# Sums over the partitions in a hybrid residual block: LayerNorm's mean and variance and the first FFN norm's sum by two float32r matmuls instead of one f32 matmul

## The chip, the cores and the metric

The kernel runs on one core of one Trainium2 chip. The metric is device time in microseconds, the median of several runs. The profile names the engines PE (matmul), PEld (weight load, of the same engine), DVE (VectorE), ACT (ScalarE), POOL (GpSimd) and SP (SyncE, which issues DMAs).

## What is computed

One trunk layer on x (1024 positions, 1024 channels), f32 in and out:

```python
h = rms_norm(x, norm_mix_g) * (1.0 + sc1) + sh1
b_s, c_s, v_s, v_c, gl_c, gate_br = split(h @ w_in)
y_a = (b_s * causal_dwconv(c_s * v_s, conv_short_w)) @ w_short_out
u = causal_dwconv(v_c * sigmoid(gl_c), conv_conf_w) + conv_conf_b
y_b = silu(layer_norm(u, conf_ln_g, conf_ln_b)) @ w_conf_out
g_a, g_b = split(sigmoid(gate_br))
x = x + g1 * ((g_a * y_a + g_b * y_b) @ w_o)
h2 = rms_norm(x, norm_ffn_g) * (1.0 + sc2) + sh2
a, bgate = split(h2 @ w_ffn_in)
x = x + g2 * ((silu(a) * bgate) @ w_ffn_out)
return rms_norm(x, final_norm_g)
```

The shifts, scales and gates (sh1, sc1, g1, sh2, sc2, g2) come from a product of silu(c) with w_ada. The change concerns three places where a sum over the channels is needed: the mean and the variance in `layer_norm`, and the sum of squares in the RMSNorm ahead of the FFN.

## The kernel before, in words

Everything is held transposed: channels lie on the 128 partitions (8 blocks of 128, KC = 8), positions on the free axis, in two halves of 512 (H). A product therefore has weights of 128x128 as the stationary side and tiles of 128x512 as the moving side.

Products run in float32r, in three parts. Each operand is split into a high part (a cast on ACT) and a low part (a subtraction on DVE, of some weights on POOL): `split_w` (L220 to L231; casts at L226, subtractions at L227) for weights, `t_split` (L419) and `q_split` (L839; casts L848, subtractions L850) for tiles. `mm3` (L372) then adds high by high (L380), high weight by low tile (L381) and low weight by high tile (L383). Most products save one in eight by a Strassen-like scheme of seven products in the order of PRODUCTS ("1265734"); some operands of these are sums of weight blocks, made at L304. One product of such a set on PE is 24 matmuls.

The stages in order, with where they lie in the trace: the combined input projection, with the causal convolution of width 31 on DVE beside it; from 565 us the fourteen products of `w_short` (`ya_order`, L1045), with LayerNorm on DVE and ACT beside them; the product with `w_conf` (tile `yb`, from 645 us); the product with `w_o` (tile `mix`, from 732 us), whose second half of positions runs beside the first half's FFN norm; the FFN; the last norm.

A sum over channels has two steps: the 8 channel blocks are added up elementwise, and the 128 partitions of the result are then summed by one matmul with a 128x128 tile `ones` as the stationary side, which leaves the sum on every partition of a PSUM tile. Before the change all these sums take the f32 tile as it is, in an f32 matmul. The ones at issue:

- `ln_mean` (L930), behind the first product of `ya_order`, for both halves: `tot[h]`, which POOL adds up at L923, is summed at L934 into a PSUM tile `mu`, and ACT scales it into SBUF at L936. `ln_square` (L941) then subtracts the mean (L945), squares on ACT (L947) and adds up on DVE (L951), for one channel block behind each product.
- `ln_rstd` (L953), behind the eleventh product: `sqs[h]` is summed at L957 into a PSUM tile `var`, for both halves, and the reciprocal root follows (L431 on ACT, L436 to L438 on DVE). `act_b` (L977) uses it, for the operands `zs` of the next product.
- `norm_2_first` (L1119), behind the first `mix` block of the second half: `norm_start` (L536) sums `sums[0]` at L540. `sums[0]` has been added up at L1102 from the squares of L1096.

Tiles come from pools. `mu` and `var` lie in a pool of two PSUM tiles ("ps2"), which the copies `y` (L1025) of the second product of `ya_order` also use. The pool "gs" holds six f32 tiles of 128x512 in SBUF: gates on their way (`ga`, `gb`), squares, reciprocal roots, the tiles `xr` of `mix`, and from L834 on four q tiles (`q01`) that stay until they have been split as q7. A tile that is asked for when all buffers are taken waits for one to come free.

The order of the instructions on each engine is set ahead of the run by a planner: it follows the order of the code, but where an instruction isn't ready by the planner's own model of times, it lets a later one of the same engine past. `tc.issue_after(ins)` pins an instruction behind another one on the same engine. On the chip each engine then goes through its list in order, with semaphores between the engines.

`fill` (L179) is a tile that nothing reads, of FILL f32 columns; it takes up room between the constants and the other pools.

Of the kernel before, what the change touches and what calls it, by code (L numbers as in the profile page):

```python
# [36 lines left out]
F32R = mybir.dt.float32r  # L37
AF = mybir.ActivationFunctionType
ALU = mybir.AluOpType

P = 128
D = 1024
T = 1024
H = 512
# [76 lines left out]
PIECES = [(0, 512), (512, 256), (768, 256)]  # L121


FILL = 248


@with_exitstack
def block_kernel(ctx: ExitStack, tc: tile.TileContext, x0, xT, c, vecs, ada, w_first, w_plain, w_duals,
                 w_short, w_conf, w_o, w_fi, w_fo, w_last, outT):
    nc = tc.nc  # L130

    def pool(name, bufs, **kw):
        return ctx.enter_context(tc.tile_pool(name=name, bufs=bufs, **kw))
# [10 lines left out]
    cp = pool("const", 1)  # L144
# [8 lines left out]
    gsp = pool("gs", 6)  # L153
# [4 lines left out]
    def ps_tile(name):  # L158
        return psp.tile([P, H], F32, tag="ps", name=name)

    def ps2_tile(name):
        return ps2p.tile([P, H], F32, tag="ps2", name=name)

    def hl_tile(name, dt=F32R):
        return tp.tile([P, H], dt, tag="t", name=name)
# [7 lines left out]
    def f32(t):  # L173
        return t.bitcast(F32)
# [3 lines left out]

    nc.gpsimd.memset(fill.tile([P, FILL], F32, name="fill"), 0.0)  # L179

# [2 lines left out]
    cs = cp.tile([P, D], F32, name="cs")  # L183
    ones = cp.tile([P, P], F32, name="ones")
    nc.vector.memset(ones, 1.0)
    eps1 = cp.tile([P, 1], F32, name="eps1")
    nc.vector.memset(eps1, EPS)
    eps2 = cp.tile([P, 1], F32, name="eps2")
# [227 lines left out]
    def t_pair(name):  # L416
        return hl_tile(name + "h"), hl_tile(name + "l")
# [9 lines left out]
    def rstd_start(ss, eps, name, n=H, tile_of=g_tile):  # L427

        r, t = tile_of(name + "r")[:, :n], tile_of(name + "t")[:, :n]
        ss = ss[:, :n]  # L430
        act = nc.scalar.activation(r, ss, AF.Abs_reciprocal_sqrt, bias=eps)  # L431
        return ss, eps, r, t, act.ins

    def rstd_end(ss, eps, r, t, exp):

        nc.vector.scalar_tensor_tensor(out=t, in0=r, scalar=-0.5, in1=r, op0=ALU.mult, op1=ALU.mult)  # L436
        nc.vector.scalar_tensor_tensor(out=t, in0=ss, scalar=eps, in1=t, op0=ALU.add, op1=ALU.mult)
        rstd_end.ins = nc.vector.scalar_tensor_tensor(out=r, in0=t, scalar=1.5, in1=r, op0=ALU.add, op1=ALU.mult).ins  # L438
        return r
# [81 lines left out]
    def squares_x(src, acc=None, clock=(), tile_of=g_tile):  # L521

        for i, t in enumerate(src):
            sq = tile_of("sq")
            act = nc.scalar.activation(sq, t, AF.Square, scale=1.0 / 32.0)
            if acc is None:
                acc = sq
            else:
                add = nc.vector.tensor_tensor(acc, acc, sq, ALU.add)
                if i in clock:  # L530
                    keep_clock(keep_clock.ins, 1, sq)
                    keep_clock(keep_clock.ins, 1, wide=True)
        squares_x.ins = act.ins, add.ins
        return acc

    def norm_start(acc, name, n=H, tile_of=g_tile, ss_tile=ps_tile):  # L536
        ss = ss_tile("ss")
        acc = acc if isinstance(acc, list) else [acc]
        for t in acc:
            norm_start.ins = nc.tensor.matmul(ss[:, :n], ones, t, start=t is acc[0], stop=t is acc[-1]).ins  # L540
        return rstd_start(ss, eps1, name, n, tile_of)
# [20 lines left out]
    def gate(b, j, h, ps):  # L562
        sig = g_tile("sig")
        nc.scalar.activation(sig, ps, AF.Sigmoid)
        nc.scalar.dma_start(gate_dram[b, j][:, halves[h]], sig)

    def keep_clock(ins, n, src=None, wide=False):

        t = ps2_tile("clock")
        lhs, src = (ones_r[:, :P], ones_r) if wide else (ones, ones if src is None else src[:, :P])  # L570
        for _ in range(n):
            with tc.issue_after(ins) if ins else ExitStack():
                ins = nc.tensor.matmul(t[:, : src.shape[-1]], lhs, src, start=True, stop=True).ins
        keep_clock.ins = ins
# [15 lines left out]
    ones_r = s_tile("ones_r", F32R)  # L590
    nc.vector.memset(f32(ones_r), 1.0)
    keep_clock(None, CLOCK[0], wide=True)
    for s, row in zip(halves, c_rows):
        silu = nc.scalar.activation(row[:1], crow[:, s], AF.Silu)
# [331 lines left out]
    tot = [hl_tile(f"tot{h}", dt=F32) for h in range(2)]  # L926
# [3 lines left out]
    def ln_mean():  # L930
        mu = []
        for h in range(2):
            mps = ps2_tile("mu")
            nc.tensor.matmul(mps, ones, tot[h], start=True, stop=True)  # L934
            mu.append(hl_tile(f"mu{h}", dt=F32))
            nc.scalar.activation(mu[h], mps, AF.Copy, scale=1.0 / D)  # L936
        return mu

    sqs = [None, None]
# [13 lines left out]
    def ln_rstd(sqs):  # L953
        rs = []
        for h in range(2):
            var = ps2_tile("var")
            nc.tensor.matmul(var, ones, sqs[h], start=True, stop=True)  # L957
            rs.append(rstd_start(var, eps2, f"rl{h}"))
        return [rstd_end(*r) for r in rs]

# [84 lines left out]
    for i, (d, m) in enumerate(ya_order):  # L1045
        product(ya_banks[d], m, tq[m], ya_evacs[d], onto="2")
        if q_steps:
            q_steps.pop(0)()
        if i == 0:
            mu = ln_mean()  # L1050
        elif i <= KC:
            ln_square(i - 1)
        elif i == KC + 2:
            rl = ln_rstd(sqs)
            act_b(0, 0)
# [9 lines left out]
    for h in range(2):  # L1065
# [3 lines left out]
        gs = []  # L1069
# [34 lines left out]
    def h2_of(k, h, r2, hi_lo=None):  # L1104

        t = x1[k][:, halves[h]]
        nc.vector.scalar_tensor_tensor(out=t, in0=t, scalar=aff2[:, k : k + 1], in1=r2, op0=ALU.mult, op1=ALU.mult)
        if hi_lo:
            hi, lo = hi_lo
            nc.scalar.activation(hi, t, AF.Identity, bias=modc(24 + k))  # L1110
            nc.vector.scalar_tensor_tensor(
                out=lo, in0=t, scalar=modc(24 + k), in1=f32(hi), op0=ALU.add, op1=ALU.subtract
            )
        nc.scalar.activation(t, t, AF.Identity, bias=modc(24 + k))
        return t
# [2 lines left out]
    ts = {m: [None] * (KC // 2) for m in PRODUCTS}  # L1118
    def norm_2_first():  # L1119

        r2 = rstd_end(*norm_start(sums[0], "r2"))
        for k in range(KC):
            ts["12"[k // KH]][k % KH] = hl = t_pair(f"h2{k}")
            h2_of(k, 0, r2, hl)
# [34 lines left out]
    sums = {}  # L1159
    for h in range(2):  # L1160
        for i in range(KC):
            mix(i, h)
            if h == 0:
                load_b(32 + i)
            if (h, i) == (0, KC - 1):
                modulation_of(*loaded.pop())
            if h == 1 and i == 0:
                for k in range(KC):
                    affine(aff2, k, 32, vec, V_GFFN)
                norm_2_first()  # L1170
            if h == 1 and i in S2_AT:
                next(in_units[1]["begin"])
# [121 lines left out]
    ss = ps_tile("ss")  # L1294
    r2 = None
# [6 lines left out]
    r2 = rstd_end(*r2)  # L1302
# [49 lines left out]
    n = 2 * GROUP * P  # L1352
# [98 lines left out]
    for i in range(len(PIECES)):  # L1451
        acc, sqs = sqs[0] if i else None, []
# [84 lines left out]
```

## Time and profile before

| what | value |
|---|---|
| median of 3 runs | 1471.18 us (1470.85 to 1472.19) |
| span of the profiled execution | 1469.8 us; its time outside the profile isn't listed |
| granted PE clock, mean | 0.998 |
| f32 sums of the mean, L934 | 4 records, 571.0 to 572.3 us |
| f32 sums of the variance, L957 | 4 records, 627.3 to 628.8 us |
| f32 sum of the first FFN norm, L540 `ss<-xr` | 2 records, at 781.6 us |

Times within the trace are microseconds from the start of the span. Of an f32 matmul the trace shows two records, each with its own weight load. Records of PE overlap: a matmul is still draining when the next one begins, so what one costs is read from the distance between starts and not from its busy time. A number in brackets behind a row is the engine's idle time ahead of it, and what ended it.

### The profile page before, as it was taken

Reading aid. Unit: us, or ns where it says so; the run is one execution under the profiler, and the core shown is the slowest. Engines: PE = TensorE matmul, PEld = TensorE weight load, DVE = VectorE, ACT = ScalarE, POOL = GpSimd, SP = SyncE. Lnnn points to the kernel's source line nnn. Section 1 sums busy time; section 2 is a strip of 40 time slices with the busy share of each in tenths; the row PEclk is TensorE's granted clock in tenths of the full one; section 3 lists DMA queues with packets and bytes.
Section 4 is the critical chain, followed back from the end, with each engine's and each line's share of the span. In section 5 each row is a group of like instructions: output and inputs, shape, how many; then the busy total and the mean of one; then the engine's idle time right before and its main releaser. Section 6 shows DMA issues by size and latency. Waiting matters only on the chain.

```text
span 1469.8 us, 17768 instructions
## 1 busy us (share of the span) xinstructions
PE 1459.0 (99%) x6447; PEld 1197.9 (81%) x6447; DVE 1178.7 (80%) x1625; ACT 615.0 (42%) x896; POOL 515.7 (35%) x464
## 2 busy tenths in 40 slices
PE   9999999999999999999999999999999999999997
PEld 5888888888888888888888888888888888888887
DVE  8999888887998969999688798777777765676755
ACT  5753433333433346455235474444444443222325
POOL 0046677767777771111022002101111115435005
PEclk9999999999999999999999999999999999999999
DMA  9412213222222258376596336654555449999403
GB/s 373 165 59 72 101 58 129 72 86 101 101 67 78 93 205 303 115 239 215 194 315 221 106 106 233 221 170 163 168 185 173 158 154 373 341 287 280 139 15 115
DMA packets 83913, 247.97 MB, mean 169 GB/s; under 512 B 9665, under 2 KB 11713, under 8 KB 83826
## 3 DMA queue, kind: packets, MB, share of 16 engines
q1 hardware_dynamic: 43072, 138.63, 28.3%
q0 software_dynamic: 37008, 95.63, 19.8%
q10 hardware_dynamic: 3746, 12.59, 2.3%
q8 instruction: 50, 0.82, 0.2%
q14 instruction: 37, 0.30, 0.1%
HBM read 184.41 MB, written 62.39 MB: 168 GB/s over the span
## 4 chain that ended last, share of the span: by engine, by line
PE 97%; DVE 1%; POOL 0%; issue 0%; ACT 0%; POOLq 0%; DVEq 0%
PE bank L383 12%; PE bank L380 12%; PE bank L381 12%; PE x L381 8%; PE x L383 8%; PE x L380 7%; PE z L380 4%; PE z L383 4%; PE z L381 4%; PE y L381 3%; PE y L380 3%; PE y L383 3%; PE mix L383 2%; PE mix L380 2%; PE yb L383 2%; PE yb L380 2%
## 5 line engine op out<-in xcount | busy, mean ns | idle before, releaser
L226 ACT CAST wh<-raw 128x1024 fp32r<-128x1024 f32 (+2 forms) x253 | 255.2, 1010 | 454.9 <-PE bank L381 129.9
L227 POOL TENSOR_TENSOR wl<-raw,wh 128x1024 fp32r<-128x1024 f32 x84 | 204.8, 2446 | 82.1 <-ACT wh L226 82.1
L227 DVE TENSOR_TENSOR wl<-raw,wh 128x1024 fp32r<-128x1024 f32 (+2 forms) x169 | 193.6, 1146 | 37.4 <-ACT wh L226 36.1
L902 DVE SCALAR_TENSOR_TENSOR c<-diff,vec,c 128x512 f32<-128x512 f32 x232 | 171.0, 752 | 4.4
L1250 POOL DMA_DIRECT2D hid<-stage x71 | 37.9, 534 | 345.4 <-DVE stage L421 341.1
L380 PE MATMUL bank<-th,wh 128*128 128x512 f32 x288 | 112.0, 389 | 0.0
L381 PE MATMUL bank<-tl,wh 128*128 128x512 f32 x288 | 112.0, 389 | 0.0
L383 PE MATMUL bank<-th,wl 128*128 128x512 f32 x288 | 112.0, 389 | 0.0
L902 DVE SCALAR_TENSOR_TENSOR c<-u,wsum,c 128x512 f32<-128x512 f32 x112 | 84.3, 753 | 2.6
L420 ACT CAST stage<-g 128x512 fp32r<-128x512 f32 x62 | 38.4, 622 | 84.0 <-DVE g L1239 41.9
L246 POOL TENSOR_TENSOR raw<-raw 128x1024 f32<-128x1024 f32 x12 | 29.2, 2433 | 125.1 <-DVE wl L227 87.7
L421 DVE TENSOR_TENSOR stage<-g,stage 128x512 fp32r<-128x512 f32 x62 | 42.4, 689 | 26.9 <-ACT stage L420 26.8
L381 PEld LDWEIGHTS bank<-tl,wh 128*128 128x128 f32 x288 | 54.1, 188 | 11.3
L383 PEld LDWEIGHTS bank<-th,wl 128*128 128x128 f32 x288 | 54.1, 188 | 11.2
L380 PEld LDWEIGHTS bank<-th,wh 128*128 128x128 f32 x288 | 54.1, 188 | 11.2
L1276 POOL DMA_DIRECT2D th<-hid x71 | 38.1, 537 | 52.8 <-PE x L383 29.3
L380 PE MATMUL x<-th,wh 128*128 128x512 f32 x144 | 56.1, 390 | 0.1
L383 PE MATMUL x<-th,wl 128*128 128x512 f32 x144 | 56.0, 389 | 0.0
L381 PE MATMUL x<-tl,wh 128*128 128x512 f32 x144 | 56.0, 389 | 0.0
L246 DVE TENSOR_TENSOR raw<-raw 128x1024 f32<-128x1024 f32 (+1 forms) x17 | 19.2, 1129 | 42.2 <-DMA raw<-in_w_fi 31.6
L380 PE MATMUL yb<-zsh,wh 128*128 128x512 f32 x128 | 49.8, 389 | 0.0
L381 PE MATMUL yb<-zsl,wh 128*128 128x512 f32 x128 | 49.8, 389 | 0.0
(811 smaller groups left out, 4243.9 us busy)
## 6 DMA issues: line engine op xcount, KB each, us to landing
hid<-stage POOLq DMA_DIRECT2D x71, 512.0 KB, 4.6
raw<-in_w_fi SPq DMA_DIRECT2D x54, 512.0 KB, 4.4
raw<-in_w_duals SPq DMA_DIRECT2D x48, 512.0 KB, 3.5
th<-hid POOLq DMA_DIRECT2D x71, 256.0 KB, 5.7
tl<-hid POOLq DMA_DIRECT2D x71, 256.0 KB, 5.7
ada<-in_ada SPq DMA_DIRECT2D x24, 512.0 KB, 5.5
raw<-in_ada SPq DMA_DIRECT2D x24, 512.0 KB, 4.5
raw<-in_w_fo SPq DMA_DIRECT2D x24, 384.0 KB, 5.8
```

The lines of the kernel that those rows point to most:

```text
L226: hi = nc.scalar.copy(wh, raw)
L227: lo = lo_engine.tensor_tensor(wl, raw, f32(wh), ALU.subtract)
L246: eng.tensor_tensor(a["s1"], a["21"], a["22"], ALU.add)
L380: nc.tensor.matmul(ps, wh, xh, start=first, stop=False, skip_group_check=again)
L381: nc.tensor.matmul(ps, wh, xl, start=False, stop=False, skip_group_check=again)
L383: mm3.ins = nc.tensor.matmul(ps, wl, xh, start=False, stop=last, skip_group_check=again).ins
L420: t_split.act = nc.scalar.copy(hi, src).ins
L421: t_split.ins = nc.vector.tensor_tensor(lo, src, f32(hi), ALU.subtract).ins
L902: tap.ins = nc.vector.scalar_tensor_tensor(out=out, in0=src[:, s : s + H], scalar=wt, in1=acc, op0=ALU.mult, op1=ALU.add).ins
L1250: nc.gpsimd.dma_start(hid_dram[key], s)
L1276: nc.gpsimd.dma_start(t, hid_dram[key][:, s])
```

## The change

A helper `parts_sum` is added. It splits the tile into a high and a low float32r part (cast on ACT, subtraction on DVE), both in buffers of "gs", and sums them by two float32r matmuls into one PSUM tile. It replaces the f32 matmul at the five places named. Its stationary tile is a new constant `ones_c`, of 128 f32 columns, set by POOL; FILL becomes smaller by as many. The sums at L540 that belong to the other norms, and those at L1437, remain as they were.

```diff
-FILL = 248
+FILL = 120
...
+    ones_c = cp.tile([P, P], F32R, name="ones_c")
+    nc.gpsimd.memset(f32(ones_c), 1.0)
...
+    def parts_sum(ss, src):
+
+        hi, lo = (gsp.tile([P, H], F32R, tag="gs", name=n) for n in ("sum_h", "sum_l"))
+        nc.scalar.copy(hi, src)
+        nc.vector.tensor_tensor(lo, src, f32(hi), ALU.subtract)
+        nc.tensor.matmul(ss, ones_c, hi, start=True, stop=False)
+        nc.tensor.matmul(ss, ones_c, lo, start=False, stop=True)
...
             mps = ps2_tile("mu")
-            nc.tensor.matmul(mps, ones, tot[h], start=True, stop=True)
+            parts_sum(mps, tot[h])
...
             var = ps2_tile("var")
-            nc.tensor.matmul(var, ones, sqs[h], start=True, stop=True)
+            parts_sum(var, sqs[h])
...
     def norm_2_first():
 
-        r2 = rstd_end(*norm_start(sums[0], "r2"))
+        ss = ps_tile("ss")
+        parts_sum(ss, sums[0])
+        r2 = rstd_end(*rstd_start(ss, eps1, "r2"))
```

## The prediction

> **What bounds the kernel now.** I read the page first: the engines' busy shares and the chain that ended last.
>
> ```profile
> PE 1459.0 (99%) x6447; PEld 1197.9 (81%) x6447; DVE 1178.7 (80%) x1625; ACT 615.0 (42%) x896; POOL 515.7 (35%) x464
> PE 97%; DVE 1%; POOL 0%; issue 0%; ACT 0%; POOLq 0%; DVEq 0%
> ```
>
> TensorE (PE) carries 97% of the chain, so at first sight each microsecond of matmul taken away is a microsecond won. But the share is a mean over stages. The five sums that change lie at 571 (mean), 627 (variance) and 781 us (first FFN norm), so I asked for the busy times of the stretches around the first two, and then for what the weight loads waited for between 599 and 617 us.
>
> ```profile
> 572.00:600.00 28.00, 28.00 (x124) 22.80 (x123) 27.82 (x40) 19.17 (x33) 2.18 (x4) 1.00 0.62 214
> 600.00:617.00 17.00, 17.00 (x76) 13.68 (x74) 17.00 (x25) 7.16 (x10) 2.15 (x4) 1.00 0.37 124
> 617.00:629.00 12.00, 12.00 (x51) 9.42 (x51) 12.00 (x17) 6.48 (x10) 1.28 (x3) 1.00 0.45 134
> 629.00:632.00 3.00, 3.00 (x14) 2.30 (x13) 1.74 (x3) 2.60 (x4) 0.87 (x2) 1.00 0.81 231
> ```
>
> ```profile
> PEld bank L383 <- DVE wl L227: 0.6, 2, 0.4
> ```
>
> The columns are the stretch and its length, then busy time of PE, PEld, DVE, ACT and POOL, the granted clock, and DMA. From 572 to 629 us VectorE (DVE) has no room: 27.82 of 28, 17.00 of 17, 12.00 of 12. And PE has already caught it up there: twice a weight load waits for the low part of a weight that DVE has just split. Here **PE and DVE bound the kernel together**, and the change takes from the one and gives to the other. ACT has a third free.
>
> **PE's side.** The rows of the matmuls around the three places (start, busy, engine, line):
>
> ```profile
> 583.65 0.39 PE L380 MATMUL bank<-q6h,wh 128*128 128x512 f32 x1
> 583.88 0.39 PE L381 MATMUL bank<-q6l,wh 128*128 128x512 f32 x1
> 584.10 0.39 PE L383 MATMUL bank<-q6h,wl 128*128 128x512 f32 x1
> 584.33 0.39 PE L380 MATMUL bank<-q6h,wh 128*128 128x512 f32 x1
> 584.55 0.39 PE L380 MATMUL y<-q2h,wh 128*128 128x512 f32 x1
> ```
>
> ```profile
> 571.01 1.88 PE L934 MATMUL mu<-tot,ones 128*128 128x512 f32 x4
> 572.95 0.39 PE L381 MATMUL bank<-q,wh 128*128 128x512 f32 x1
> ```
>
> ```profile
> 627.48 1.88 PE L957 MATMUL var<-sq,ones 128*128 128x512 f32 x4
> 629.42 0.39 PE L381 MATMUL bank<-q7l,wh 128*128 128x512 f32 x1
> ```
>
> ```profile
> 781.55 1.02 PE L540 MATMUL ss<-xr,ones 128*128 128x512 f32 x2
> 782.64 0.39 PE L381 MATMUL mix<-mg01l,wh 128*128 128x512 f32 x1
> ```
>
> Matmuls overlap, so the price is the step between starts: 583.65 to 584.55 is four steps, 0.225 us each. The two f32 sums of the mean begin at 571.01; the second matmul behind them begins at 572.95, one step earlier the first really got going, so they cost 572.95 - 0.225 - 571.01 = 1.71 us. The variance: 629.42 - 0.225 - 627.48 = 1.71. The FFN sum: 782.64 - 0.225 - 781.55 = 0.86. Together 4.28 us. The new sums are ten matmuls of the float32r kind, which all products here are: 10 x 0.225 = 2.25. **Saved on PE: 2.03 us** (0.81 + 0.81 + 0.41). That is all that this change can win directly.
>
> **What is added.** Five casts on ACT, five subtractions on DVE, and per sum the path cast, subtraction, matmul where PE took the f32 tile at once. Steps, from the same operations on the same shape:
>
> ```profile
> 582.95 2.19 ACT L848 CAST q3h<-q 128x512 fp32r<-128x512 f32 x4
> 587.14 2.49 DVE L850 TENSOR_TENSOR q<-q,q3h 128x512 fp32r<-128x512 f32 x4
> ```
>
> ACT: about 0.55 a cast, DVE: about 0.62 a subtraction. The casts are covered by ACT's idle third.
>
> *Mean.* Its two subtractions are 1.24 us on a DVE without a gap. One could be cheaper: the sums' input is done early, and a cast and a subtraction could be issued ahead. But what DVE does then is dear:
>
> ```profile
> 550.09 3.44 POOL L923 TENSOR_TENSOR tot<-tot,u 128x512 f32<-128x512 f32 x2
> 550.61 6.88 DVE L425 SCALAR_TENSOR_TENSOR q<-q,q 128x512 f32<-128x512 f32 x4
> 553.50 2.83 POOL L227 TENSOR_TENSOR wl<-raw,wh 128x1024 fp32r<-128x1024 f32 x1
> ```
>
> Four operations take 6.88 us, 1.72 each, while POOL works. The Trainium skill (SBUF — State Buffer, "Who interferes with whom") says that a DVE instruction with two SBUF inputs and a GpSimd instruction that reads SBUF lock each other out for the whole instruction; these rows agree, and by it an early subtraction would cost 1.72 instead of 0.62, 1.1 us more in the sum. Bounds of the two subtractions: 0 (if LayerNorm's own later work gives way and the weight splits do not) to 3.44. I take 1.24, by the rows nearest to 572 us. So at the two waits around 600 and 616 us the weight comes 1.24 us later than now; PE's 0.81 is spent waiting there, as PE has no margin. **Mean: +1.2 us.**
>
> *Variance.* Two more subtractions, 1.24 us:
>
> ```profile
> 625.66 0.69 DVE L951 TENSOR_TENSOR sq<-sq 128x512 f32<-128x512 f32 x1
> 626.26 1.22 DVE L304 TENSOR_TENSOR raw<-raw 128x1024 f32<-128x1024 f32 x1
> 627.51 1.05 ACT L226 CAST wh<-raw 128x1024 fp32r<-128x1024 f32 x1 [0.68 <-DVE raw L304]
> 631.08 0.69 DVE L436 SCALAR_TENSOR_TENSOR rl0t<-rl0r 128x512 f32<-128x512 f32 x1 [1.26 <-ACT rl0r L431]
> ```
>
> DVE idles 1.26 us before 631.08, waiting for the variance itself, so the second half's subtraction is covered: if that cover is gone it costs 0.62. But the weight that PE uses right behind the sums is cast until 628.56 (627.51 + 1.05), released by DVE's L304, and the first matmul on it falls, two steps counted back from 629.42, at 628.97: 0.4 us behind the cast. So the shorter sums win at most 0.4 of their 0.81 here; and the first half's subtraction may stand ahead of L304 and push the cast back by 0.62. Bounds -0.4 to +0.6; I take **+0.2**, nearer to the upper end, as DVE is full until 629 us.
>
> *First FFN sum.* The last addition ends at 778.57 + 0.69 = 779.26, and both engines then wait for PE:
>
> ```profile
> 778.57 0.69 DVE L1102 TENSOR_TENSOR xr<-xr 128x512 f32<-128x512 f32 x1
> 781.75 0.75 DVE L1092 SCALAR_TENSOR_TENSOR x<-mix,mod,xr 128x512 f32<-128x512 f32 x1 [2.50 <-PE mix L383]
> 779.28 0.20 ACT L457 ACTIVATE rs<-ones 128x1 f32<-128x1 f32 x1
> 781.53 1.05 ACT L226 CAST wh<-raw 128x1024 fp32r<-128x1024 f32 x1 [2.04 <-PE mix L381]
> ```
>
> Cast 779.5 to 780.1, subtraction to 780.8, PE there at 781.55: hidden, with 0.7 us to spare, and PE keeps **-0.41**. If the cast is queued behind ACT's 781.53 work, PE waits until about 784.5, +2.9 us; that end belongs to the second rival.
>
> *The constants.* `ones_c` and the smaller FILL are set by POOL at the start (a 0.30 us memset becomes two), while PE's first matmul waits for DVE:
>
> ```profile
> 0.74 0.30 POOL L179 MEMSET fill<- 128x248 f32 x1 [0.29 <-POOLq L1526]
> 1.62 4.63 PE L573 MATMUL clock<-ones_r 128*128 128x512 f32 x10 [1.62 <-DVE ones_r L591]
> ```
>
> Nothing, at most a tenth.
>
> **Sum.** +1.2 + 0.2 - 0.4 = +1.0 us on the span of 1469.8. The profiled execution's own time isn't listed; the median of the runs, 1471.18, lies 1.38 above the span, and I carry that over: **1472.2 us**, +0.07%. Of no change a measurement of this kernel can tell about 0.2%, 2.9 us, so this is "the same".
>
> **Rivals.** *The subtractions hide.* If DVE puts off LayerNorm's own operations and not the weight splits, PE keeps all 2.03: 1469.2, still within 0.2%. For it: DVE's idle 1.26 us. Against: 0.18 us of idle time in the 57 us before. 14%.
>
> *PE waits at the mean's second half.* This one ends slower. Both parts come from the six-buffer pool "gs". Four of the six then hold q tiles, the first half's parts take the other two, and the second half needs buffers that come free with the q7 subtractions, or once PE has added the first half.
>
> ```profile
> 581.00 1.08 ACT L936 ACTIVATE mu<-mu 128x512 f32<-128x512 f32 x2
> 581.96 1.08 ACT L1025 COPY y<-bank 128x512 f32<-128x512 f32 x2
> 583.52 1.29 DVE L850 TENSOR_TENSOR q7l<-q,q7h 128x512 fp32r<-128x512 f32 x2
> ```
>
> If the subtraction comes behind the last q7 (584.8), the parts are there at 585.4. A PE order that has the sum behind the second product (24 steps, 5.4 us, behind 571.6) then stands from 577.0 to 585.4: 8.4 us, with 2.03 kept, as DVE has caught up meanwhile: +6.4, 1477.6. Behind PE stand all products, and ACT's copies of y need the two PSUM buffers of mu, so they slip too. It decides from a wait of 5 us on (5 - 2.03 = 2.9). Against it: the order is made by a planner which lets later matmuls past: in the rows above, four of q6 run before y, for which PE would have waited, and ACT's copies of y ended at 583.04, 1.5 us before PE read them. So its errors seem to be one or two microseconds. A long stand could cost more than itself: the first ten matmuls above step at 0.46 us, twice the 0.225, and as long a start again would cost 4.63 - 2.25 = 2.4 us. The Trainium skill (TensorE: Matmul & The Clock Gate, "Part 1") has PE fall to half its clock after an idle window of about 3.4 us; by it this rival would be some 1.7 us dearer (my estimate: 3.4 us at half speed), and no row here has such a gap in mid-kernel to show it. With the FFN sum's 2.9 us and a doubled cost of the subtractions in the same case: 28%, 1475 to 1479.
>
> *A reshuffle helps.* Adding instructions may reorder the rest. Faster than 2.9 us would need all of PE's 2.03 and most of the waits that PE has left (0.6 above, and the one below): 1468.0. 6%.
>
> ```profile
> PEld x L381 <- DVE t4l L421: 0.9, 1, 0.9
> ```
>
> That the matmuls would not be cheaper speaks against every product row; I give it nothing.
>
> **How the numbers follow.** Forecast 52%, of which I count 6 as slower (DVE's upper bounds, 3.44 instead of 1.24, with +0.6 at the variance and -0.4: +3.6, 1474.8); hiding 14%; PE's wait 28%; reshuffle 6%. Faster 6%, the same 46 + 14 = 60%, slower 28 + 6 = 34%. Range: from 1469.0, just under the hiding case, to 1477.5, most of PE's wait; left out are the reshuffle below and some 14% above. The likeliest case's own range is 1470.8 (nothing but the FFN sum's -0.4) to 1474.8.
>
> **What the profile after would show.** PE: the three f32 groups gone, ten matmuls of 0.39 us at a 0.225 step. PEld's wait for `wl` between 599 and 617 us grown from 0.6 to about 2.6 us: right; unchanged: the hiding case. DVE in 572 to 617 still full. Around 781 us no wait of PE, `ss` 0.41 shorter; a wait for the helper's `lo` there would prove me wrong. A wait of PE or PEld for a part of the mean's sum over 5 us is the slower rival. If DVE shows idle time between 572 and 617, my bound was the wrong one.

## The result, and the profile after

The changed kernel takes 1473.79 us (median of 21 runs, 1472.49 to 1476.59), the kernel before beside it 1471.64 (21 runs, 1470.85 to 1473.15): a ratio of 1.0014 with a 95% interval of 1.0008 to 1.0021, that is 1.2 to 3.1 us slower. The profiled execution's span went from 1469.8 to 1470.7 us at a granted clock of 0.999; that +0.9 is smaller than the change's price, because PE's stops near 1261 to 1267 us, 0.7 us in the profile before, happen to be missing in this one. Forecast were +1.0 us and 1472.2. So the direction of the sum and two of its three terms hold, and one term was too small.

The page of the changed kernel, busy shares and the chain that ended last:

```profile
PE 1457.7 (99%) x6447; PEld 1197.3 (81%) x6447; DVE 1182.5 (80%) x1630; ACT 617.6 (42%) x901; POOL 515.8 (35%) x465
PE 93%; DVE 4%; issue 1%; DMA 1%; ACT 1%; POOL 0%; POOLq 0%; DVEq 0%; ACTq 0%
```

PE still fills 99% of the span, with 1.3 us less of work; DVE has 3.8 us more. In the chain, PE's share fell from 97 to 93% and DVE's rose from 1 to 4%: the chain leaves PE for DVE in more places. It says neither where nor how much: 3% of the span are 44 us, and the kernel is some 2 us slower.

The stretches around the mean and the variance (columns as before: PE, PEld, DVE, ACT, POOL, granted clock, DMA):

```profile
572.00:600.00 28.00, 26.40 (x115) 21.22 (x114) 27.80 (x39) 20.14 (x34) 2.18 (x4) 1.00 0.62 221
600.00:617.00 17.00, 17.00 (x76) 14.08 (x75) 17.00 (x26) 6.29 (x10) 2.15 (x4) 1.00 0.36 124
...
629.00:632.00 3.00, 2.54 (x11) 1.77 (x11) 2.69 (x3) 1.67 (x3) 0.00 (x0) 1.00 0.77 274
632.00:645.00 13.00, 12.98 (x57) 10.09 (x56) 10.65 (x16) 8.15 (x10) 2.15 (x4) 1.00 0.66 223
```

DVE is as full as before up to 629 us (27.80 of 28, 17.00 of 17, and 12.00 of 12 in the stretch left out), as forecast. But PE has a hole of 1.6 us in the first stretch, where it had none, and one of 0.5 us from 629 to 632. And behind the variance DVE itself is idle for 2.35 of 13 us: there an engine that had work to do was kept from it.

What PE's weight loads waited for between 572 and 732 us (line, what released it, us in total, times, longest):

```profile
PEld mu L575 <- DVE sum_l L573: 2.0, 1, 2.0
PEld bank L382 <- ACT wh L228: 0.9, 1, 0.9
PEld yb L382 <- DVE gb L1083: 0.8, 1, 0.8
PEld bank L382 <- ACT cv L993: 0.4, 1, 0.4
...
```

One wait of 2.0 us stands at the mean's own sum, for the low part of its second half; the next three stand at the variance and behind it. The wait for `wl` at 600 and 616 us, which I expected to grow from 0.6 to 2.6 us, is gone.

**Where the time went.** The way to place a loss is to follow one and the same matmul through both traces. Before:

```profile
565.57 0.39 PE L380 MATMUL bank<-q1h,wh 128*128 128x512 f32 x1
...
610.91 0.39 PE L380 MATMUL bank<-q4h,wh 128*128 128x512 f32 x1
...
732.60 0.39 PE L380 MATMUL mix<-mg00h,wh 128*128 128x512 f32 x1
```

After:

```profile
565.38 0.39 PE L382 MATMUL bank<-q1h,wh 128*128 128x512 f32 x1
...
612.01 0.39 PE L382 MATMUL bank<-q4h,wh 128*128 128x512 f32 x1
...
734.70 0.39 PE L382 MATMUL mix<-mg00h,wh 128*128 128x512 f32 x1
```

The shifts are -0.19, +1.11 and +2.10 us. What lies ahead of the first of them is hardly part of the change (two profiles of the changed kernel, `after` and e12 below, differ by 0.9 us there), so the differences count: between q1 and q4 lies the mean (+1.30), between q4 and the first `mix` the variance (+0.99), and from there to the first `x<-h20` the FFN sum (-0.41). Below, every kernel's shifts against the trace of before, at the first matmul of each of these products; the experiments follow.

| kernel | q1 (565.57) | q4 (610.91) | mix (732.60) | x<-h20 (820.53) | mean | variance | FFN sum |
|---|---|---|---|---|---|---|---|
| after | -0.19 | +1.11 | +2.10 | +1.69 | +1.30 | +0.99 | -0.41 |
| e12, after once more | +0.74 | +1.70 | +3.35 | +2.94 | +0.96 | +1.65 | -0.41 |
| e1, mean alone | -0.40 | +0.83 | +0.60 | +0.60 | +1.23 | -0.23 | 0.00 |
| e2, variance alone | -0.39 | +0.12 | +1.13 | +1.13 | +0.51 | +1.01 | 0.00 |
| e3, FFN sum alone | -0.42 | -0.48 | -0.60 | -1.01 | -0.06 | -0.12 | -0.41 |
| e4, mean, lows apart | +0.27 | +0.46 | +1.23 | +1.23 | +0.19 | +0.77 | 0.00 |
| e5, mean's load only | +0.34 | +1.20 | +1.18 | +1.19 | +0.86 | -0.02 | +0.01 |
| e6, e4 on POOL | -0.39 | +0.04 | +0.82 | +0.82 | +0.43 | +0.78 | 0.00 |
| e8, variance, lows apart | +0.45 | +0.81 | +1.52 | +1.52 | +0.36 | +0.71 | 0.00 |
| e9, e4 with less DVE work | -0.37 | -0.38 | -0.31 | -0.31 | -0.01 | +0.07 | 0.00 |
| e10, variance's load only | -0.16 | -0.21 | -0.20 | -0.20 | -0.05 | +0.01 | 0.00 |
| e11, high parts only | +0.60 | +1.02 | +0.13 | -0.52 | +0.42 | -0.89 | -0.65 |
| e13, casts first, and FFN sum | +0.64 | +0.58 | +0.10 | -0.19 | -0.06 | -0.48 | -0.29 |

The columns name the stretch, not the cause: in e4 and e6 part of the mean's cost shows up only behind q4. Kernels without any change at the mean still differ in its column by up to half a microsecond (e2: +0.51, e3: -0.06), by their `wl` waits of 600 and 616 us; and the two profiles of the changed kernel differ by 0.34 at the mean and 0.66 at the variance. So a single entry of these two columns under 0.7 us is not to be read by itself. The FFN column is steadier: -0.41 in three profiles.

**The mean, close up.** PE in the changed kernel, then DVE's subtractions of both halves and ACT's cast of the second:

```profile
576.75 0.40 PE L574 MATMUL mu<-sum_h,ones_c 128*128 128x512 f32 x1
...
578.13 0.39 PE L385 MATMUL bank<-q2h,wl 128*128 128x512 f32 x1
580.11 0.50 PE L575 MATMUL mu<-sum_l,ones_c 128*128 128x512 f32 x1 [1.60 <-DVE sum_l L573]
580.45 0.40 PE L382 MATMUL bank<-q2h,wh 128*128 128x512 f32 x1
580.68 0.40 PE L383 MATMUL bank<-q,wh 128*128 128x512 f32 x1
```

```profile
557.27 0.68 DVE L573 TENSOR_TENSOR sum_l<-tot,sum_h 128x512 fp32r<-128x512 f32 x1
...
579.38 0.68 DVE L573 TENSOR_TENSOR sum_l<-tot,sum_h 128x512 fp32r<-128x512 f32 x1
```

```profile
573.32 0.64 ACT L572 CAST sum_h<-tot 128x512 fp32r<-128x512 f32 x1
```

The first half's parts are made early, the second half's 22 us later, although its input was ready by 553.5 us (POOL's row in the prediction, the same here). DVE, which has no gap there, takes the second at 579.38, and PE, whose last step ahead of that sum begins at 578.13, stands until 580.11. That is the place that the slower rival named, with a quarter of its forecast stand of 8.4 us.

**The variance, close up.** The roots and the low part of the first operand of `yb`, before:

```profile
630.36 0.69 ACT L431 ACTIVATE rl0r<-var,eps 128x512 f32<-128x512 f32 x1
630.94 0.68 ACT L431 ACTIVATE rl1r<-var,eps 128x512 f32<-128x512 f32 x1
639.65 0.69 DVE L413 TENSOR_TENSOR zsl<-cv,zsh 128x512 fp32r<-128x512 f32 x1 [0.18 <-ACT zsh L412]
```

After (the five rows of ACT follow each other on that engine without another operation between them; then rows of DVE):

```profile
631.42 1.28 ACT L433 ACT_TABLE_LOAD   x1 [1.33 <-PE var L575]
632.71 0.69 ACT L433 ACTIVATE rl0r<-var,eps 128x512 f32<-128x512 f32 x1
633.30 0.61 ACT L572 CAST sum_h<-sq 128x512 fp32r<-128x512 f32 x1
634.56 1.05 ACT L228 CAST wh<-raw 128x1024 fp32r<-128x1024 f32 x1 [0.65 <-DMA raw<-in_w_short]
635.51 0.69 ACT L433 ACTIVATE rl1r<-var,eps 128x512 f32<-128x512 f32 x1
```

```profile
626.99 0.69 DVE L961 TENSOR_TENSOR sq<-sq 128x512 f32<-128x512 f32 x1
...
633.94 0.69 DVE L573 TENSOR_TENSOR sum_l<-sq,sum_h 128x512 fp32r<-128x512 f32 x1 [2.25 <-ACT sum_h L572]
...
644.04 0.68 DVE L415 TENSOR_TENSOR zsl<-cv,zsh 128x512 fp32r<-128x512 f32 x1
```

Before, the two roots follow each other within 0.6 us. Now the second half's cast, whose input is ready at 627.68, stands in ACT's queue behind the first half's root until 633.30, and with it behind that half's cast, subtraction, two matmuls and the table load of 1.28 us. Its subtraction comes 2.25 us of idle DVE time later, the second root 4.57 us later than before (635.51 against 630.94), and the first operand for `yb` 4.4 us later (644.04 against 639.65). The second root doesn't even come directly behind its sum: between them ACT has the cast of a weight, which waited for its DMA. Before, that cast came behind both roots. DVE's idle time of 1.26 us, in which I had put the subtraction, was not filled: from 629 to 645 us DVE is idle for 2.66 us, before for 1.86.

**The FFN sum, close up.** PE, then DVE:

```profile
783.65 0.40 PE L574 MATMUL ss<-sum_h,ones_c 128*128 128x512 f32 x1
...
784.12 0.39 PE L382 MATMUL mix<-mg01h,wh 128*128 128x512 f32 x1
```

```profile
781.94 0.69 DVE L573 TENSOR_TENSOR sum_l<-xr,sum_h 128x512 fp32r<-128x512 f32 x1 [1.04 <-ACT sum_h L572]
```

The subtraction ends at 782.63, 1.0 us before PE comes to the sum; that takes 784.12 - 783.65 = 0.47 us on PE, where it was 0.86. No wait; -0.41 as forecast.

### The profile page after: what moved, and what is told of

It is laid out like the page before. It is cut to its first block, busy times and chain, and to the rows that moved or that the text cites. A ratio compares the mean times of both kernels' runs of the same rounds, so it can differ in the third digit from the quotient of the medians.

```text
span 1470.7 us, 17781 instructions
## 1 busy us (share of the span) xinstructions
PE 1457.7 (99%) x6447; PEld 1197.3 (81%) x6447; DVE 1182.5 (80%) x1630; ACT 617.6 (42%) x901; POOL 515.8 (35%) x465
## 4 chain that ended last, share of the span: by engine, by line
PE 93%; DVE 4%; issue 1%; DMA 1%; ACT 1%; POOL 0%; POOLq 0%; DVEq 0%; ACTq 0%
PE bank L382 11%; PE bank L385 11%; PE bank L383 11%; PE x L383 8%; PE x L385 8%; PE x L382 7%; PE z L382 4%; PE z L385 4%; PE z L383 4%; PE y L382 3%; PE y L385 3%; PE y L383 3%; PE mix L383 2%; PE mix L382 2%; PE mix L385 2%; PE lead L385 1%
## 5 line engine op out<-in xcount | busy, mean ns | idle before, releaser
L385 PE MATMUL yb<-zsh,wl 128*128 128x512 f32 x128 | 49.8, 389 | 0.0
```

The costliest lines, as they stand in the source:

```text
L385: mm3.ins = nc.tensor.matmul(ps, wl, xh, start=False, stop=last, skip_group_check=again).ins
```

## The experiments

The theory after the result: **load** at the mean (DVE is full, so 1.24 us of subtractions come out as PE's wait, wherever that is) and, at the variance, either the same load or the **delay** of the roots. The rival at the mean: **buffers** (the low part of the second half is late because the pool "gs" has no buffer for it, and with buffers the loss would vanish).

### e1: the mean alone

```diff
-            parts_sum(var, sqs[h])
+            nc.tensor.matmul(var, ones, sqs[h], start=True, stop=True)
...
-        ss = ps_tile("ss")
-        parts_sum(ss, sums[0])
-        r2 = rstd_end(*rstd_start(ss, eps1, "r2"))
+        r2 = rstd_end(*norm_start(sums[0], "r2"))
```

> Only the mean is summed in parts; variance and FFN sum are f32 as before. Buffer theory (the second half's parts wait for a buffer of gs, and PE stands for its low part): PE waits about 2 us for sum_l near 580 us, 0.81 us are won, and about +1.1 us are left in the product stage of w_short, 1.0007 of before. Load theory (the two subtractions on a full DVE are the price, wherever they stand): the same +1.1 us, so this run tells the theories apart only by where the wait lies. If the 0.8 us that the changed kernel lost around 695 us came from the late variance, it is not here; if from the mean, it is, and the ratio is 1.0013.

Measured: 1472.18 us, ratio 1.0003 (0.9995 to 1.0012); PE's shift +1.23 to q4 and +1.00 to `mix`. From 572 to 620 us the weight loads wait 2.0 us for the mean's `sum_l`, as in the changed kernel, and 0.4 us for a copy `y` of ACT.

Waits of 2.4 us in place of 0.6, less the 0.81 that PE saves: +1.0. So the mean's term is there without the others, at the same place as in the changed kernel. The loss behind 629 us isn't there: it belongs to the variance.

### e2: the variance alone

The mean and the FFN sum are put back as above; `parts_sum(var, sqs[h])` stays.

> Only the variance is summed in parts. Expected +0.2 to +0.5 us from the waits for the parts between 628 and 635 us. If the late variance (its root came 4 us later) is what costs 0.8 us at 695 us, then +1.0 to +1.3 us in all, 1.0008; if not, 1.0002.

Measured: 1472.94 us, ratio 1.0012 (1.0003 to 1.0021). From q4 to `mix` +1.01; another +0.51 lies ahead of q4, where this kernel is the one before. The second root is late here too (630.94 before), with nothing changed at the mean, and so is the operand (643.48, before 639.65):

```profile
631.26 0.69 ACT L433 ACTIVATE rl0r<-var,eps 128x512 f32<-128x512 f32 x1
...
634.96 0.68 ACT L433 ACTIVATE rl1r<-var,eps 128x512 f32<-128x512 f32 x1
```

### e3: the FFN sum alone

Mean and variance are put back; the FFN sum keeps its parts.

> Only the first FFN norm's sum is in parts. Both theories: the parts are hidden behind PE, 0.41 us won, 0.9997 of before; in the trace no wait of PE at the sum.

Measured: 1472.13 us, ratio 1.0001 (0.9992 to 1.001); in the trace -0.41 between `mix` and `x<-h20`, and no wait at the sum. The time alone can't show 0.4 us; the trace does.

### e4: the mean, its low parts in another tile

e1, with the low parts in a tile of the pool of `diff`, which is free there, so that only the high parts need "gs":

```diff
+        los = diffp.tile([P, T + CK - 1], F32R, tag="diff", name="diff")
         for h in range(2):
             mps = ps2_tile("mu")
-            parts_sum(mps, tot[h])
+            parts_sum(mps, tot[h], los[:, halves[h]])
```

> As e1, but the low parts lie in the tile of the convolution's differences, which is free by then, so that both halves find buffers and the parts of both are made by 559 us. Buffer theory: PE does not wait at the sums, the 0.81 us stay won, 0.9995 of before. Load theory: the two subtractions are still on a DVE without a gap, so the weights at 600 and 616 us come 1.2 us later than before, PE's waits for wl between 599 and 617 us grow from 0.6 to about 2.6 us, and the kernel is 1.2 us slower than before, 1.0008.

Measured: 1472.55 us, ratio 1.0004 (0.9995 to 1.0013). Both subtractions are now done early, and PE waits for neither sum. DVE, and PE's waits from 572 to 620 us:

```profile
550.93 4.68 DVE L427 SCALAR_TENSOR_TENSOR q<-q,q 128x512 f32<-128x512 f32 x4
555.53 3.48 DVE L575 TENSOR_TENSOR diff<-tot,sum_h 128x512 fp32r<-128x512 f32 x2
```

```profile
PEld bank L382 <- DVE ma L752: 0.9, 1, 0.9
PEld bank L385 <- DVE wl L229: 0.9, 2, 0.5
PEld bank L382 <- ACT wh L228: 0.8, 1, 0.8
```

So buffers decide *where* PE waits: 2.0 us at the sum became 2.6 us at other places between 572 and 620, for DVE's other work and for a cast. They don't decide *how much*: +0.96 to `mix`, where e1 has +1.00. The rival has fallen, the load stands.

### e5: the mean's load without its use

The kernel before, with a cast and a subtraction behind each f32 sum of the mean, whose results nobody reads:

```diff
             nc.tensor.matmul(mps, ones, tot[h], start=True, stop=True)
+            parts_only(tot[h])
```

> The kernel before, with the mean's casts and subtractions added and their results used by nothing; the sums stay f32. Load theory: DVE sets the time of this stage, so its two more subtractions cost the same whether PE's sums are short or long; about +1.0 us by 732 us against the start of the w_short products, as in e1 and e4, 1.0007 of before. Wait theory (the price is PE standing for the parts): nothing waits for them, 0.0 us, 1.0000.

Measured: 1473.72 us, ratio 1.0013 (1.0004 to 1.0022); +0.84 to `mix`. PE's waits from 572 to 620 us, 0.6 before:

```profile
PEld bank L383 <- DVE wl L227: 1.4, 2, 1.0
```

Here PE does exactly the work of before, and loses 0.8 us at the two `wl` waits where I had put the loss. The added work alone brings it. It is casts on ACT and subtractions on DVE together; that DVE is the one that pays is read from the engine that PE waits for, from DVE's 17.00 of 17 us between 600 and 617, and from e9. With the 0.81 of PE's saving (e1, e4) or without it (e5) the loss is nearly the same, 0.8 to 1.0 us, as it must be where DVE sets the pace: what PE saves, it waits.

### e6: the mean's subtractions on POOL

e4, with `nc.gpsimd.tensor_tensor` for the subtraction.

> As e4, with the mean's two subtractions on POOL, which is idle from 556 us on. Three answers for the shift by 732 us: if PE bounds the stage, its 0.81 us are won now, -0.8; if DVE bounds it and POOL's work costs DVE nothing, 0.0 (PE waits out what it has won); if a POOL subtraction holds DVE's two-input instructions up for its own length, as the rows around 553 us say, about +1, as when DVE does it itself.

Measured: 1472.72 us, ratio 1.0005 (0.9996 to 1.0014); +1.21 to `mix`, no cheaper than on DVE. POOL, and DVE beside it:

```profile
552.93 3.44 POOL L575 TENSOR_TENSOR diff<-tot,sum_h 128x512 fp32r<-128x512 f32 x2
```

```profile
558.04 3.50 DVE L427 SCALAR_TENSOR_TENSOR q<-q,q 128x512 f32<-128x512 f32 x4
```

In e1 the same four operations of DVE take 2.48 us. DVE has 1.24 us less to do and loses about 1.0 of it here, where POOL's later work now lies beside it. That is the third answer of the expectation, by another way than it says: POOL's subtractions stretch nothing that wasn't stretched before (the first four operations take 6.88 us as in the kernel before), but they push POOL's next operation (a weight's subtraction, from 556.33 us) on to others.

### e8: the variance, its low parts in another tile

e2, with the edit of e4 in `ln_rstd`.

> As e2 (variance alone), with the low parts in the tile of the convolution's differences, so that the second half's parts need not wait for a buffer of gs. Buffer theory for the variance: the second half's root comes 2 us earlier than in e2 and the +1.0 us that e2 showed by 732 us fall to 0.2 or less. Load theory: +1.0 as in e2, since the two subtractions still stand on DVE.

Measured: 1472.45 us, ratio 1.0004 (0.9995 to 1.0013); +0.71 from q4 to `mix`, +1.07 in all. The second root is as late as in e2, again behind a weight's cast that waited for its DMA:

```profile
634.17 1.05 ACT L228 CAST wh<-raw 128x1024 fp32r<-128x1024 f32 x1 [1.81 <-DMA raw<-in_w_short]
635.12 0.69 ACT L433 ACTIVATE rl1r<-var,eps 128x512 f32<-128x512 f32 x1
```

So buffers aren't the price of the variance. The number agrees with the load, but e10 shows that it isn't the load either.

### e9: e4 with less work on DVE

e4, with one step left out: block 1's squares are not added to the variance's sum, which takes two additions, 1.2 us, off DVE between the mean and the variance.

```diff
             if j == 0:
                 sqs[h] = sq
-            else:
+            elif j > 1:
                 nc.vector.tensor_tensor(sqs[h], sqs[h], sq, ALU.add)
```

> As e4, without the two additions that take the second channel block's squares into the variance (its output is therefore another one). This gives DVE back about the 1.2 us that the two subtractions took. Load theory: e4's waits near 594 and 617 us shrink and the shift by 732 us falls from +1.0 to between -0.6 and 0.0. Wait theory: nothing of what PE waits for at the sums has changed, +1.0 stays.

Measured: 1471.16 us, ratio 0.9992 (0.9983 to 1.0001); +0.06 to `mix`. With DVE's load back to that of before, the mean in parts costs nothing, although its casts are still there. It gives nothing either: PE still waits 1.5 us from 572 to 620 where it waited 0.6 before, each time for DVE, and its 0.81 go there.

### e10: the variance's load without its use

The kernel before, with `parts_only(sqs[h])` behind each f32 sum of the variance.

> The kernel before, with the variance's casts and subtractions added behind its f32 sums and used by nothing. Load theory for the variance: the shift from the 610 us products to the start of mix is about the +1.0 us of e2, 1.0007 of before. Delay theory (the price is the root that comes 2 to 4 us later, because the sums wait for the parts): the root isn't delayed by parts here, so 0.0 to +0.3 us, 1.0001.

Measured: 1471.98 us, ratio 1.0003 (0.9994 to 1.0012); +0.01 from q4 to `mix`. Nothing waits for the parts now. ACT's roots:

```profile
630.12 0.69 ACT L431 ACTIVATE rl0r<-var,eps 128x512 f32<-128x512 f32 x1
631.21 0.69 ACT L431 ACTIVATE rl1r<-var,eps 128x512 f32<-128x512 f32 x1
```

The roots begin within 0.3 us of those in the kernel before (630.36 and 630.94), and PE loses nothing. Casts and subtractions do fit beside the variance, as I had said; what costs is that the root has to wait for them.

### e11: high parts only

The low parts are left out of all five sums, so each is one cast and one float32r matmul.

> All five sums by one float32r matmul of the high part alone; the low parts are left out, so DVE gets no work more and PE saves 0.64 us a sum, 3.2 us in all. If PE bounded these stages: -2.5 us by 732 us and -3.2 at the end, 0.9978. If DVE bounds the mean's stage: PE waits out most of the mean's 1.27 us at the weights of 600 and 616 us; by 732 us between 0.0 and -1.0, then -0.64 at the FFN sum; in all -0.6 to -1.6 us, 0.9992.

Measured: 1470.21 us, ratio 0.9995 (0.9987 to 1.0004). PE saves 5 x 0.63 = 3.2 us and keeps 1.1 (+0.60 at q1, -0.52 at `x<-h20`): all of the FFN sum's 0.65, 0.89 at the variance, and nothing at the mean (+0.42), though DVE has no more to do there than before. PE's wait between 572 and 620 us:

```profile
PEld bank L382 <- ACT vz L1036: 1.8, 1, 1.8
```

ACT's copy of `vz` at 600 us stands behind a cast that it used to precede; the planner's order has changed. The sum agrees with a stage bound by DVE, but this wait is of another kind, and I don't count it as proof: here PE lost its saving without one subtraction more on DVE. Whether the added casts or only the other order brought that about, no run shows.

### e12: the changed kernel once more

No edit; a second profile of it.

> The changed kernel once more, for a second profile. By 732 us +2.3 us against the start of the w_short products as in its first profile, if the waits near 580, 629 and 695 us are the program's; parts of it that differ by some tenths are the run's.

Measured: 1474.07 us beside 1471.40, ratio 1.0018 (1.0008 to 1.0027). The two longest waits from 572 to 732 us:

```profile
PEld mu L575 <- DVE sum_l L573: 1.7, 1, 1.7
PEld bank L382 <- ACT cv L993: 1.6, 1, 1.6
...
```

The wait at the mean and the losses behind the variance come back, in other shares (+0.96, +1.65, -0.41, together +2.20, after +1.88). A likely source of the larger loss at the variance, not tested, is that the weight's cast ahead of the second root waited 1.88 us for its DMA, in the first profile 0.65; the root came at 637.32.

### e13: the variance's casts ahead of the roots, and the FFN sum

e8, with both casts and both subtractions written ahead of the loop of sums and roots; and the FFN sum in parts. The mean has its f32 sums. (`parts_of` is the first half of `parts_sum`, `add_up` its two matmuls.)

```diff
+        los = diffp.tile([P, T + CK - 1], F32R, tag="diff", name="diff")
+        parts = [parts_of(sqs[h], los[:, halves[h]]) for h in range(2)]
         for h in range(2):
             var = ps2_tile("var")
-            parts_sum(var, sqs[h], los[:, halves[h]])
+            add_up(var, *parts[h])
             rs.append(rstd_start(var, eps2, f"rl{h}"))
```

> The mean is back on its f32 sums; the variance and the first FFN sum keep their parts. The variance's low parts lie in another tile, and both casts and both subtractions are written ahead of the two roots, not each half's behind the other half's root. In the three kernels with the variance in parts so far, ScalarE's second cast stood behind the table load and the first root (631.75 to 633.30 us), 5 us after its input was ready, and the second root began 2.8 to 4.0 us after the first. Theory 1 (the second cast's place in ScalarE's queue is the price of the variance): the second root follows the first within 0.7 us, the first low part for yb is done by 642 us, and PE's shift from the q4 product (610.9) to the first mix is at most +0.3 us, against +0.71 with the parts apart. Theory 2 (any path of cast, subtraction and matmul in front of the root costs that much): the shift stays at +0.7 to +1.0. Both expect -0.4 at the FFN sum. Total: -0.9 to -0.1 us by theory 1, +0.3 to +0.6 by theory 2; neither can be told from 1471.4 by the time alone, so PE's shifts decide.

Measured: 1470.43 us (11 runs) beside 1471.66, ratio 0.9996 (0.9987 to 1.0005). ACT:

```profile
626.26 0.62 ACT L574 CAST sum_h<-sq 128x512 fp32r<-128x512 f32 x1
...
627.73 0.62 ACT L574 CAST sum_h<-sq 128x512 fp32r<-128x512 f32 x1
...
631.71 0.69 ACT L433 ACTIVATE rl0r<-var,eps 128x512 f32<-128x512 f32 x1
632.30 0.68 ACT L433 ACTIVATE rl1r<-var,eps 128x512 f32<-128x512 f32 x1
```

The second cast comes 4 us earlier than in e8, the second root right behind the first (632.30, in e8 635.12). From q4 to `mix` PE's shift is -0.48, where e8 has +0.71. The same instructions in another order are 1.2 us cheaper, about twice what two profiles of one kernel differ by: the second cast's place in ACT's queue was the price of the variance, and theory 2 has fallen. Part of the price may go by way of the weight's cast: in e13 it stands behind both roots, so its wait for the DMA holds up neither. No run separates this from the rest. Both roots are still 1.35 us later than before, 0.6 of it from what lies ahead of q1, and PE keeps 0.48 of the 0.81 that the shorter sums save. The FFN sum gave 0.3 here, as PE waits 0.3 for its low part. In all, PE is 0.83 us ahead from q1 on; the time can't be told from that of before, so this isn't shown to be a faster kernel.

## Why the prediction was right, and where it was wrong

*What bounds.* Right: PE and DVE together. e5 (the added work without its use: +0.84) and e9 (as much taken off DVE again: +0.06) show it, and DVE is full from 572 to 629 us in the changed kernel as well.

*PE's saving of 2.03 us.* The steps are right: a sum of two parts takes 0.47 us, two steps of 0.23, where one f32 sum took 0.86. Of the 2.03, 0.41 reach the end.

*The mean, +1.2.* Right in size: +1.30, +0.96 and, alone, +1.23 to q4. Wrong in place: I had said that PE would wait for `wl` at 600 and 616 us. In e5 it does; in the changed kernel it waits at the sum itself, because the second half's parts come late, and then, PE having stood for 2 us, DVE has the splits for 600 and 616 us done in time. This is the slower rival's mechanism at a quarter of its size: 2.0 us, under the 5 from which it would have decided. The rival's cause, the buffers, sets the place and not the sum (e4). Without that stop the load costs 0.84 (e5) and 0.96 (e4), somewhat under the forecast 1.24; that the changed kernel comes so near to it is partly chance.

*The dear early subtraction.* I took 3.44 us as the upper bound, 1.72 for each subtraction beside POOL. In e4 both were issued there and took 3.48, so each duration was as foretold, and the Trainium skill's rule that two such instructions lock each other out (SBUF — State Buffer, "Who interferes with whom") agrees with it. But the sum didn't become dearer: the four q operations that now come ahead of them took 4.68 us, not 6.88, so that the six together need 8.16, 1.28 more than the four alone. POOL's work slows whatever DVE does beside it, and POOL had no more to do (its next operation only began 1.74 us later), so an operation of DVE that moves there pushes another one out. The bound was too high by this.

*The variance, +0.2 between -0.4 and +0.6.* This term was too small, and its reasoning failed: +0.99 and +1.65 in the two profiles of the changed kernel, +1.01 alone. Two sentences of mine are wrong in it: that the casts are covered by ACT's idle third, and that the second half's subtraction is covered by DVE's idle time. Both looked at free time on an engine (e10: the load does fit, +0.01). Neither looked at the order: the code makes the second half's cast *behind* the first half's root, and ACT keeps that order. So its input lay ready for 5.6 us, the second root and the operands behind it came 4.4 to 4.6 us late, and PE lost 1.0 to 1.65 us by it in small waits (for a weight's cast, `cv`, the sum's parts, `gb`). The planner also put a weight's cast, which waits for a DMA, ahead of the second root. e13 shows the order's price by turning it around. Had I written down ACT's sequence through the helper's two calls, I would have seen it: the helper carries one cast and one root per turn of the loop.

*The FFN sum, -0.4.* Right: -0.41 in the changed kernel, e3 and e12, with 1.0 us to spare where I had counted 0.7.

*The constants, nothing.* Nothing that can be told from what differs between two runs of one kernel (the changed one and e12 are 0.9 us apart at q1).

*The sum.* With the variance at its measured +1.0 in place of +0.2, the forecast would have been +1.8; the trace has +1.88, and the runs +2.1 (1.2 to 3.1). Of the 1.6 us between 1472.2 and 1473.79, 0.46 is the base: I counted from the median of three runs, 1471.18, and that of 21 is 1471.64. What differs near 1261 to 1267 us (stops of PE: 0.7 us before, none and 1.0 in the two profiles of the changed kernel, 1.9 in e3) belongs to no part of the change.

## What to carry to other kernels

Where a second engine is full beside the one that the page calls the bound, price a change by what it adds to the second; what the first saved here, it waited. When a helper puts a cast and a subtraction in front of something that the next operations need, write down the order of each queue through all its calls, not only the free time of the engine: here a cast behind a root cost PE about 1.2 us that the same cast ahead of it didn't, and what the planner had put between them waited for a DMA besides. And follow one matmul through two traces: a difference of 0.4 us, too small for the measured time, can still be found and placed that way, once two traces of one kernel have shown how much such a figure varies by itself.

## What the runs showed of the hardware

Beside POOL's two-input operations DVE's durations are shared time, not a price per instruction: with POOL at work, two subtractions more cost 1.28 us in all although each took 1.74 (e4). By my estimate from these rows, four of DVE's six operations were stretched to 1.72 us, as many as before, and the other two took 0.62: 8.12 us, where the rows have 8.16. And moving the two subtractions to POOL took 1.24 us from DVE and gave back 1.0, by stretching four of its operations from 2.48 to 3.50 us (e6).

PE stood for 2.0 us in the middle of the kernel; the next steps were 0.34 and 0.23 us at a granted clock of 1.00, so a stop of this length cost about 0.1 us beyond itself. No run has a longer one between 20 and 1455 us, so the slow start that the prediction had feared behind a long stop stays open.
